# A convolution norm with its low parts on VectorE, its gates' sigmoids in one piece and the Silu table loaded ahead; a last norm whose gain is multiplied in half by half

## The chip, the cores and the metric

The kernel runs on one core of a Trainium2 chip. A core has TensorE (PE, with its weight loads shown apart as PEld), VectorE (DVE), ScalarE (ACT), GpSimd (POOL), SyncE (SP, which issues the transfers here) and 16 DMA engines. The metric is the device time of one execution in microseconds. The kernel before took 1084.35 us in the median of three runs (1084.35, 1085.1 and 1082.03). A fourth execution was profiled.

## The reference, cut to what matters

A sequence of 256 tokens of width 1024 in float32 passes one hybrid block (attention, a matrix LSTM and an MLP) and then two layers of a second block. The change touches the second block and the norm behind it:

```python
for l in range(2):
    h = rms_norm_2(x, norm1_g[l]) * (1.0 + scale1) + shift1
    z = h @ w_in[l]
    ...
    y_attn = o.reshape(b, s, ATTN_W) @ w_attn_o[l]
    ga, gb = jnp.split(z[..., C_OFF:G_OFF], 2, axis=-1)
    u = ga * jax.nn.sigmoid(gb)
    u = causal_depthwise_conv(u, dw_conv_w[l], dw_conv_b[l])       # 31 taps, 512 channels
    u = jax.nn.silu(layer_norm(u, conv_ln_g[l], conv_ln_b[l]))
    y_conv = u @ w_conv_o[l]
    g_attn, g_conv = jnp.split(jax.nn.sigmoid(z[..., G_OFF:]), 2, axis=-1)
    mixed = (g_attn * y_attn + g_conv * y_conv) @ w_out[l]
    x = x + (1.0 + gate1) * mixed
    h2 = rms_norm_2(x, norm2_g[l]) * (1.0 + scale2) + shift2
    f_gate, f_up = jnp.split(h2 @ w_ffn_in[l], 2, axis=-1)
    x = x + (1.0 + gate2) * ((jax.nn.silu(f_gate) * f_up) @ w_ffn_out[l])
return rms_norm_2(x, final_g)
```

`rms_norm_2` multiplies by the reciprocal root of the mean of the squares and by a gain; `layer_norm` does so after taking off the mean, and adds a bias.

## The kernel before, in words

Every large product runs as three TensorE passes over float32 parts. A weight piece of 128x1024 is loaded as `raw`; ScalarE copies it to a rounded high part `whi` (L202), and the low part `wlo` = raw minus high part is made by GpSimd (L206) or VectorE (L208). Which of the two is settled when the program is written out, by a running sum in `split`: each piece adds `rot["pool"]` to `rot["n"]`; when the sum reaches 1, the piece goes to GpSimd and 1 is taken off, else to VectorE. With `rot["pool"]` at 0.75 every fourth piece goes to VectorE, with 1.0 none. Activations are split in the same way, high part on ScalarE (L589), low part on VectorE (L590).

Order. Each engine runs its own instructions in the order in which the Python program writes them; semaphores join the engines. The program writes TensorE's blocks, and after each block `tick()` gives a turn to queues of generators: `fills`, `bg`, and `pump()`, which splits the next weight pieces while fewer than 9 (`HB`) are ahead of their use. A `yield` in a generator means: the rest is written after a later block.

The second block, per layer: q, k, v and the gates' products; the attention in `attention2()` beside them; the depthwise convolution `conv()` as a `bg` generator, 31 taps on VectorE (L1251); then the four blocks "ao" (w_attn_o), the four blocks "co" (w_conv_o), then w_out, a norm, and the FFN.

The gates. The products leave the gates' input in the tile `gt` (called T in the trace), copied there at L1387. `sig(j)` (L1391) is one ScalarE sigmoid over a quarter of it, 128x1024. Two of them stand ahead of the ao blocks, the third ahead of ao block 1, the fourth ahead of ao block 2 (`SIG = (1, 2)`). After each ao block VectorE multiplies the gate into the result (L1398).

The convolution's norm, at the end of `conv()`, is written in turns between the ao blocks: mean by TensorE with a matrix of ones, mean taken off on VectorE (L1262), squares on ScalarE (L1266), their sum by TensorE (L1272), plus eps on VectorE (L1275), power -0.5 on GpSimd (L1276: "the root"), two diagonal matrices from it on ScalarE (L1279), a product with ones on TensorE that spreads the root over the partitions (L1285), four products on VectorE (L1287), and Silu on ScalarE (L1293). L589 and L590 then split the result into `uT` (called AB in the trace), which the co blocks read (TensorE L288 to L290). Between sigmoid and Silu ScalarE loads another table, an instruction of its own (ACT_TABLE_LOAD) that stands ahead of the first function that needs it. When the taps are done, `conv()` sets `rot["pool"]` from 1.0 to `LN_POOL`, 0.75.

The end. `end_all()` runs for each of two tiles of 128 tokens after the last product: per half of 512 columns gate product (L565), residual sum (L566), squares with their sum (L506); then on GpSimd eps and root (L498, L499), on VectorE x times root times `final_g` for both halves (L1468), each followed by its transfer out (L1469).

Of the kernel before, what the change touches and what calls it, by code (L numbers as in the profile page):

```python
# [43 lines left out]
TAPS_AT = 2  # L44
LOADS = 3
LN = (1, 2, 2)
SIG = (1, 2)
FDEL, ZDEL = 2, 3
RED, ROWD = 5, 8
ATT = (0, 1, 2, 4, 5, 6, 7)  # L50
# [7 lines left out]
def tile_hybrid_then_diff(ctx: ExitStack, tc: tile.TileContext, I, out: bass.AP):  # L58
# [17 lines left out]
    def st_tile():  # L76
        return sb.tile([128, 8], FT, name="st", bufs=12)

    def xn_tile(shape=(128, 1024)):
        return sb.tile(list(shape), FT, name="xn", bufs=2)  # L80
# [421 lines left out]
    def halves_of(v):  # L502
        return [v[:, n * 512:(n + 1) * 512] for n in range(2)]
# [58 lines left out]
    def post_gate(t, acc, grow, xn, sx):  # L562
        xs, g = halves_of(x[t]), halves_of(grow)
        for n in range(2):
            V.tensor_mul(acc[n], acc[n], g[n])  # L565
            V.tensor_add(xs[n], xs[n], acc[n])  # L566
            square(t, n, xn(), sx)
            if n == 0:
                yield
# [651 lines left out]
    for l in range(NL):  # L1221
        cu = sb.tile([128, 4, 286], FT, name="cu")
        G.memset(cu[:, :, 0:30], 0.0)
        attended = []
        uT = []

        def evac(t, acc):
# [14 lines left out]
        def conv():  # L1242
# [9 lines left out]
                                           cw[:, l * 4 + j, k:k + 1], sums[j], op0=OP.mult, op1=OP.add)  # L1252
                    yield
            rate["bg"] = 1
            rot["pool"] = LN_POOL
            s3 = xn_tile((128, 4, 256))
            for _ in range(LN[0]):
                yield
# [18 lines left out]
            dg = s3[:, 3, :]  # L1277
            for t in range(2):
                A.activation(dg[:, t * 128:(t + 1) * 128], ident, AF.Copy, scale=st[:, 2 + t:3 + t])  # L1279
            for _ in range(LN[2]):  # L1280
                yield
            while not attended:
# [106 lines left out]

        def sig(j):  # L1390
            A.activation(gt[:, 4 * j:4 * j + 4, :], gt[:, 4 * j:4 * j + 4, :], AF.Sigmoid)  # L1391

        sig(0)
        sig(1)
        for j in range(4):
            if j in SIG:
                sig(2 + SIG.index(j))
            b4_half("ao", oT, lambda ps, j=j: V.tensor_mul(gt[:, 2 * j:2 * j + 2, :], gt[:, 2 * j:2 * j + 2, :], ps))  # L1398
        drain_q(bg)
        rot["pool"] = POOL  # L1400
# [59 lines left out]
            yield from fin(post_gate, t, acc, g2[0], gc, bc)  # L1460

        def end_all(t, acc):
            st = st_tile()
            o = xn_tile()
            yield from post_gate(t, acc, g2[0], lambda: o, st)
            rstd2(st[:, 2:3], st, 1e-6)
            for n, (v, u, g) in enumerate(zip(halves_of(x[t]), halves_of(o), halves_of(gfin))):
                V.scalar_tensor_tensor(u, v, st[:, 2:3], g, op0=OP.mult, op1=OP.mult)  # L1468
                nc.sync.dma_start(out[0, t * 128:(t + 1) * 128, n * 512:(n + 1) * 512], u)  # L1469
            yield  # L1470

        ffn(FF2 // 256, PRE2, prefix2, up2, "fo", end_all if l == NL - 1 else to_layer(l + 1, end_layer),
# [28 lines left out]
```

## Time and profile before

| | |
|---|---|
| runs | 1084.35, 1085.1, 1082.03 us |
| profiled execution, time | 1083.16 us |
| its span in the trace | 1081.4 us |
| instructions | 17255 |
| DMA | 231.84 MB, mean 214 GB/s |

The profile covers one execution, from its first to its last instruction; 1.8 us of the execution's own time lie outside the span. In rows of the timeline the columns are: start and duration in us, engine, line, operation, output<-input by the program's names, shape; a count x2 after several equal instructions in a row, whose duration is then that of all; in brackets the idle time of the engine ahead of it and what ended that. Busy shares of engines that others don't wait for say nothing of the end. [...]

### The profile page before, as it was taken

What the parts mean: (1) busy time and instruction counts of PE and PEld (TensorE: products, weight loads), DVE (VectorE), ACT (ScalarE), POOL (GpSimd) and SP (SyncE); (2) the same over time, 40 slices, a digit from 0 to 9 for tenths busy, and PEclk for the clock granted to TensorE, in tenths of its full rate; (3) what the DMA queues carried; (4) which work ended last, traced back from release to release, by engine and by line L of the source; (5) the groups of instructions that cost most, each with busy time, mean ns of one, the idle gap of its engine ahead of it and who ended that gap; (6) DMA issues with size and microseconds to landing.
All of it is one profiled execution on the core that took longest, in us unless ns stands there. A gap on an engine that the chain in (4) does not pass through costs nothing.

```text
span 1081.4 us, 17255 instructions
## 1 busy us (share of the span) xinstructions
PE 1036.0 (96%) x6459; PEld 917.6 (85%) x6459; DVE 647.9 (60%) x1161; ACT 558.8 (52%) x933; POOL 691.5 (64%) x424
## 2 busy tenths in 40 slices
PE   8879989999998999989999999999999899999997
PEld 6667769899886789988798998888899778999995
DVE  4536556887854497834679797547873554441224
ACT  5745746444455556665643434475676545443441
POOL 2474648566575797846656665859967458566661
PEclk9989999999999999999999999999999999999999
DMA  8554545999974565546499999837635456765631
GB/s 259 169 176 130 192 146 189 345 356 362 329 268 136 167 185 165 187 156 175 132 353 318 332 343 358 299 104 214 186 127 175 137 175 224 258 224 180 198 108 39
DMA packets 169424, 231.84 MB, mean 214 GB/s; under 512 B 10215, under 2 KB 109757, under 8 KB 169339
## 3 DMA queue, kind: packets, MB, share of 16 engines
q1 hardware_dynamic: 169211, 230.71, 65.0%
q8 instruction: 51, 0.84, 0.3%
q14 instruction: 34, 0.28, 0.1%
q0 software_dynamic: 128, 0.02, 0.0%
HBM read 229.64 MB, written 1.06 MB: 213 GB/s over the span
## 4 chain that ended last, share of the span: by engine, by line
PE 75%; POOL 8%; DVE 6%; ACT 6%; issue 3%; DMA 2%; POOLq 0%; SPq 0%; DVEq 0%; ACTq 0%
PE bank L288 17%; PE bank L289 17%; PE bank L290 17%; PE bank L300 12%; POOL wlo L206 6%; PE bank L302 6%; ACT whi L202 2%; DVE bank L762 2%; DVE wlo L208 2%; DMA raw<-in_ada_w_dram 2%; PE bank L840 1%; ACT xn L506 1%; PE bank L860 1%; PE bank L531 1%; PE bank L832 0%
## 5 line engine op out<-in xcount | busy, mean ns | idle before, releaser
L206 POOL TENSOR_TENSOR wlo<-raw,whi 128x1024 fp32r<-128x1024 f32 x255 | 631.5, 2498 | 259.1 <-ACT whi L202 228.4
L202 ACT ACTIVATE whi<-raw 128x1024 fp32r<-128x1024 f32 x332 | 337.4, 1054 | 78.3 <-DMA raw<-in_w_down_dram 30.6
L288 PE MATMUL bank<-T,whi 128*128 128x256 f32 x1072 | 307.7, 287 | 2.3 <-DVE sc L773 2.3
L290 PE MATMUL bank<-T,wlo 128*128 128x256 f32 x1072 | 303.4, 283 | 0.0
L289 PE MATMUL bank<-T,whi 128*128 128x256 f32 x1072 | 303.3, 283 | 0.0
L288 PEld LDWEIGHTS bank<-T,whi 128*128 128x128 f32 x1072 | 205.1, 191 | 6.8 <-issue 3.7
L289 PEld LDWEIGHTS bank<-T,whi 128*128 128x128 f32 x1072 | 205.2, 191 | 1.1
L290 PEld LDWEIGHTS bank<-T,wlo 128*128 128x128 f32 x1072 | 205.1, 191 | 0.0
L300 PE MATMUL bank<-whi,T 128*128 128x512 f32 (+1 forms) x672 | 185.0, 398 | 7.3 <-ACT T L589 4.7
L208 DVE TENSOR_TENSOR wlo<-raw,whi 128x1024 fp32r<-128x1024 f32 x77 | 125.5, 1630 | 100.6 <-ACT whi L202 100.1
L300 PEld LDWEIGHTS bank<-whi,T 128*128 128x128 f32 x672 | 123.9, 192 | 36.6 <-ACT T L589 6.1
L762 DVE SCALAR_TENSOR_TENSOR bank<-raw,cact,bank 128x512 f32<-128x512 f32 x168 | 126.9, 755 | 7.5 <-DMA raw<-in_ada_w_dram 2.1
L288 PE MATMUL bank<-whi,AB 128*128 128x512 f32 x304 | 120.7, 397 | 0.0
L290 PE MATMUL bank<-whi,AB 128*128 128x512 f32 x304 | 120.1, 395 | 0.0
L289 PE MATMUL bank<-wlo,AB 128*128 128x512 f32 x304 | 120.0, 395 | 0.0
L302 PE MATMUL bank<-wlo,T 128*128 128x512 f32 (+1 forms) x336 | 103.8, 393 | 4.0 <-POOL wlo L206 3.0
L1251 DVE SCALAR_TENSOR_TENSOR bank<-cu,cw,bank 128x256 f32<-128x256 f32 x232 | 104.4, 486 | 4.2
L302 PEld LDWEIGHTS bank<-wlo,T 128*128 128x128 f32 x336 | 62.4, 190 | 19.9 <-POOL wlo L206 4.3
L589 ACT ACTIVATE AB<-bank 128x512 fp32r<-128x512 f32 (+1 forms) x49 | 26.0, 537 | 91.3 <-DVE bank L1449 66.2
L290 PEld LDWEIGHTS bank<-whi,AB 128*128 128x128 f32 x304 | 57.3, 188 | 13.4
L288 PEld LDWEIGHTS bank<-whi,AB 128*128 128x128 f32 x304 | 57.4, 189 | 12.0
L289 PEld LDWEIGHTS bank<-wlo,AB 128*128 128x128 f32 x304 | 57.3, 189 | 12.0
(283 smaller groups left out, 1160.5 us busy)
## 6 DMA issues: line engine op xcount, KB each, us to landing
raw<-in_w_in_dram SPq DMA_DIRECT2D x96, 512.0 KB
raw<-in_ada_w_dram SPq DMA_DIRECT2D x96, 512.0 KB
raw<-in_w_ffn_in_dram SPq DMA_DIRECT2D x88, 512.0 KB
raw<-in_w_ffn_out_dram SPq DMA_DIRECT2D x44, 512.0 KB
raw<-in_w_up_dram SPq DMA_DIRECT2D x32, 512.0 KB
raw<-in_w_down_dram SPq DMA_DIRECT2D x32, 512.0 KB
raw<-in_w_out_dram SPq DMA_DIRECT2D x24, 512.0 KB
raw<-in_w_attn_o_dram SPq DMA_DIRECT2D x8, 512.0 KB
```

What stands on the lines that cost most here:

```text
L202: A.activation(hi, r, AF.Copy)
L206: G.tensor_sub(lo, r, hi.bitcast(FT))
L208: V.tensor_sub(lo, r, hi.bitcast(FT))
L288: T.matmul(o, lh, rh, start=start, stop=False)
L289: T.matmul(o, lh, rl, start=False, stop=False)
L290: T.matmul(o, ll, rh, start=False, stop=stop)
L300: T.matmul(o, xT[:, a, k0 + kk, ts], w[0][:, kk, cs], start=start and kk == a == 0, stop=False)
L302: T.matmul(o, xT[:, 0, k0 + kk, ts], w[1][:, kk, cs], start=False, stop=stop and kk == kn - 1)
L506: A.activation(halves_of(xn)[n], halves_of(x[t])[n], AF.Square, scale=1.0 / 32, accum_out=st[:, n:n + 1])
L589: A.activation(dst_hi, full, AF.Copy)
L762: V.scalar_tensor_tensor(ada["sum"], r[:, kk, :], cact[:, k:k + 1], ada["sum"], op0=OP.mult, op1=OP.add)
L1251: V.scalar_tensor_tensor(ca[:, j, :] if k == 30 else sums[j], cu[:, j, k:k + 256], cw[:, l * 4 + j, k:k + 1], sums[j], op0=OP.mult, op1=OP ...
```

## The change

Four edits.

1. `SIG` is gone. The four sigmoids stand one behind the other ahead of the first ao block; each notes itself in a list `gated`.
2. After the taps `rot["pool"]` is 0.0 instead of 0.75, so that each low part is VectorE's (and the running sum `rot["n"]` stands still), until the diagonal matrices are written; from there on 0.75.
3. Behind the diagonal matrices `conv()` waits (in the order of writing) until four sigmoids are in `gated`, and then writes a Silu of one column of ones into an unused column of `st`. It brings the Silu table's load to this place.
4. `end_all()` is written anew: `final_g` is multiplied into half 0 as soon as that half of x is there; eps is added to half 0's sum of squares; with half 1's sum there is one addition and the root. ScalarE scales half 0 by the root, VectorE half 1 by root and gain, and both transfers are issued after these.

```diff
-SIG = (1, 2)
...
         attended = []
+        gated = []
         uT = []
...
             rate["bg"] = 1
-            rot["pool"] = LN_POOL
+            rot["pool"] = 0.0
             s3 = xn_tile((128, 4, 256))
...
             for t in range(2):
                 A.activation(dg[:, t * 128:(t + 1) * 128], ident, AF.Copy, scale=st[:, 2 + t:3 + t])
+            rot["pool"] = LN_POOL
+            while len(gated) < 4:
+                yield
+            A.activation(st[:, 4:5], ones[:, 0:1], AF.Silu)
             for _ in range(LN[2]):
                 yield
...
         def sig(j):
             A.activation(gt[:, 4 * j:4 * j + 4, :], gt[:, 4 * j:4 * j + 4, :], AF.Sigmoid)
-
-        sig(0)
-        sig(1)
+            gated.append(j)
+
         for j in range(4):
-            if j in SIG:
-                sig(2 + SIG.index(j))
+            sig(j)
+        for j in range(4):
             b4_half("ao", oT, lambda ps, j=j: V.tensor_mul(gt[:, 2 * j:2 * j + 2, :], gt[:, 2 * j:2 * j + 2, :], ps))
...
         def end_all(t, acc):
-            st = st_tile()
-            o = xn_tile()
-            yield from post_gate(t, acc, g2[0], lambda: o, st)
-            rstd2(st[:, 2:3], st, 1e-6)
-            for n, (v, u, g) in enumerate(zip(halves_of(x[t]), halves_of(o), halves_of(gfin))):
-                V.scalar_tensor_tensor(u, v, st[:, 2:3], g, op0=OP.mult, op1=OP.mult)
-                nc.sync.dma_start(out[0, t * 128:(t + 1) * 128, n * 512:(n + 1) * 512], u)
+            st, o, junk = st_tile(), xn_tile(), sc_tile()
+            xs, os, gs, fs = (halves_of(v) for v in (x[t], o, g2[0], gfin))
+            for n in range(2):
+                V.tensor_mul(acc[n], acc[n], gs[n])
+                V.tensor_add(xs[n], xs[n], acc[n])
+                A.activation(junk, xs[n], AF.Square, scale=1.0 / 32, accum_out=st[:, n:n + 1])
+                if n == 0:
+                    V.tensor_mul(os[0], xs[0], fs[0])
+                    G.tensor_scalar(st[:, 3:4], st[:, 0:1], 1e-6, None, op0=OP.add)
+                    yield
+            G.tensor_add(st[:, 4:5], st[:, 3:4], st[:, 1:2])
+            G.tensor_tensor(st[:, 5:6], st[:, 4:5], nhalf[:, 0:1], op=OP.pow)
+            A.activation(os[0], os[0], AF.Copy, scale=st[:, 5:6])
+            V.scalar_tensor_tensor(os[1], xs[1], st[:, 5:6], fs[1], op0=OP.mult, op1=OP.mult)
+            for n in range(2):
+                nc.sync.dma_start(out[0, t * 128:(t + 1) * 128, n * 512:(n + 1) * 512], os[n])
             yield
```

What this does to the order of the instructions is shown at three places. In the changed file lines up to the gates have numbers one lower (L201, L205 and L207 for the high part and for the low part on GpSimd and on VectorE), the sigmoids are L1395, the early Silu is L1283, the products by the root L1291, the gate products L1401 and the Silu itself L1297. Numbers after an underscore tell buffers apart; the piece from raw_4568 is the same in both.

ScalarE in layer 0, from the last copy of the gates' input to the first Silu, before and changed:

```order
L1391 ACT_TABLE_LOAD
L1391 ACTIVATE T16_4062<-T16_4062 128x1024 x2
L202 ACTIVATE whi_4844<-raw_4562 128x1024
L1279 ACTIVATE xn_4776<-ident_113,st_4859 128x128 x2
L1391 ACTIVATE T16_4062<-T16_4062 128x1024
L202 ACTIVATE whi_4891<-raw_4568 128x1024
L1391 ACTIVATE T16_4062<-T16_4062 128x1024
L202 ACTIVATE whi_4924<-raw_4654 128x1024
L202 ACTIVATE whi_4962<-raw_4660 128x1024
L1293 ACT_TABLE_LOAD
L1293 ACTIVATE bank_4970<-xn_3765,col_157 128x256 x2
```

```order
L1395 ACT_TABLE_LOAD
L1395 ACTIVATE T16_4062<-T16_4062 128x1024 x4
L201 ACTIVATE whi_4846<-raw_4562 128x1024
L1279 ACTIVATE xn_4776<-ident_113,st_4861 128x128 x2
L1283 ACT_TABLE_LOAD
L1283 ACTIVATE st_4861<-ones_101 128x1
L201 ACTIVATE whi_4893<-raw_4568 128x1024
L201 ACTIVATE whi_4925<-raw_4654 128x1024
L201 ACTIVATE whi_4963<-raw_4660 128x1024
L1297 ACTIVATE bank_4971<-xn_3765,col_157 128x256 x2
```

Two sigmoids went from behind the diagonal matrices to ahead of the second weight piece. The table's load went from just ahead of Silu to behind the matrices, with three weight pieces between it and Silu. Layer 1 has the same order.

VectorE in layer 0, from the mean's subtraction on, before and changed:

```order
L1262 SCALAR_TENSOR_TENSOR xn_3765<-bank_4777,xn_3765 128x1024
L1398 TENSOR_TENSOR T16_4062<-T16_4062,bank_4818 128x512
L1275 TENSOR_SCALAR st_4859<-bank_4850 128x2
L1398 TENSOR_TENSOR T16_4062<-T16_4062,bank_4865 128x512
L208 TENSOR_TENSOR wlo_4892<-raw_4568,whi_4891 128x1024
L1398 TENSOR_TENSOR T16_4062<-T16_4062,bank_4898 128x512
L1287 TENSOR_TENSOR xn_3765<-xn_3765,bank_4930 128x256 x4
```

```order
L1262 SCALAR_TENSOR_TENSOR xn_3765<-bank_4777,xn_3765 128x1024
L207 TENSOR_TENSOR wlo_4811<-raw_4468,whi_4810 128x1024
L1401 TENSOR_TENSOR T16_4062<-T16_4062,bank_4820 128x512
L207 TENSOR_TENSOR wlo_4847<-raw_4562,whi_4846 128x1024
L1275 TENSOR_SCALAR st_4861<-bank_4852 128x2
L1401 TENSOR_TENSOR T16_4062<-T16_4062,bank_4867 128x512
L1401 TENSOR_TENSOR T16_4062<-T16_4062,bank_4899 128x512
L1291 TENSOR_TENSOR xn_3765<-xn_3765,bank_4931 128x256 x4
```

Two low parts have come ahead of the addition of eps (L1275), the second of them from the weight piece that ScalarE splits after its four sigmoids. The one ahead of the products by the root is gone; in layer 0 the next low part on VectorE stands behind those products.

The same stretch of VectorE in layer 1, before and changed:

```order
L1398 TENSOR_TENSOR T16_7944<-T16_7944,bank_8768 128x512
L208 TENSOR_TENSOR wlo_8795<-raw_8524,whi_8794 128x1024
L1287 TENSOR_TENSOR xn_7647<-xn_7647,bank_8800 128x256 x4
L1398 TENSOR_TENSOR T16_7944<-T16_7944,bank_8806 128x512
L590 TENSOR_TENSOR AB_8839<-bank_8840,AB_8838 128x512
```

```order
L207 TENSOR_TENSOR wlo_8718<-raw_8433,whi_8717 128x1024
L1275 TENSOR_SCALAR st_8732<-bank_8723 128x2
L1401 TENSOR_TENSOR T16_7945<-T16_7945,bank_8738 128x512
L1401 TENSOR_TENSOR T16_7945<-T16_7945,bank_8770 128x512
L207 TENSOR_TENSOR wlo_8797<-raw_8525,whi_8796 128x1024
L1291 TENSOR_TENSOR xn_7648<-xn_7648,bank_8802 128x256 x4
L1401 TENSOR_TENSOR T16_7945<-T16_7945,bank_8808 128x512
L589 TENSOR_TENSOR AB_8841<-bank_8842,AB_8840 128x512
```

In layer 1 a low part stays ahead of the products by the root. It belongs to the second of the three weight pieces that ScalarE now splits behind the table's load; the first and the third of them are GpSimd's.

The orders of TensorE and SP are the same in both files but for names.

## Rows read from the trace of the kernel before

**Rows 1.** The page's first part: busy time, share of the span and instructions of each engine.

```profile
PE 1036.0 (96%) x6459; PEld 917.6 (85%) x6459; DVE 647.9 (60%) x1161; ACT 558.8 (52%) x933; POOL 691.5 (64%) x424
```

**Rows 2.** The waits of TensorE by what ended them, the first of them: total us, times, the longest.

```profile
PE bank L288 <- ACT AB L589: 7.8, 2, 3.9
```

**Rows 3.** Timeline of ScalarE in layer 0, from the sigmoids' table to the first two Silus.

```profile
462.50 1.28 ACT L1391 ACT_TABLE_LOAD   x1
463.79 2.01 ACT L1391 ACTIVATE T<-T 128x1024 f32<-128x1024 f32 x2
465.70 1.04 ACT L202 ACTIVATE whi<-raw 128x1024 fp32r<-128x1024 f32 x1
469.90 0.70 ACT L1279 ACTIVATE xn<-ident,st 128x128 f32<-128x128 f32 x2 [3.15 <-POOL st L1276]
470.50 1.04 ACT L1391 ACTIVATE T<-T 128x1024 f32<-128x1024 f32 x1
471.45 1.04 ACT L202 ACTIVATE whi<-raw 128x1024 fp32r<-128x1024 f32 x1
...
473.35 1.98 ACT L202 ACTIVATE whi<-raw 128x1024 fp32r<-128x1024 f32 x2
475.35 1.28 ACT L1293 ACT_TABLE_LOAD   x1
476.64 1.17 ACT L1293 ACTIVATE bank<-xn,col 128x256 f32<-128x256 f32 x2
```

**Rows 4.** Timeline of VectorE in layer 0: the addition of eps, the low part, the products by the root, the low part of the activations.

```profile
465.49 0.15 DVE L1275 TENSOR_SCALAR st<-bank 128x2 f32<-128x2 f32 x1
...
472.58 1.23 DVE L208 TENSOR_TENSOR wlo<-raw,whi 128x1024 fp32r<-128x1024 f32 x1 [3.42 <-ACT whi L202]
...
474.32 1.41 DVE L1287 TENSOR_TENSOR xn<-xn,bank 128x256 f32<-128x256 f32 x4
```

**Rows 5.** Timeline of GpSimd in layer 0, around the root.

```profile
466.82 2.40 POOL L206 TENSOR_TENSOR wlo<-raw,whi 128x1024 fp32r<-128x1024 f32 x1 [1.90 <-ACT whi L202]
469.17 0.69 POOL L1276 TENSOR_TENSOR st<-st,nhalf 128x2 f32<-128x2 f32 x1
```

**Rows 6.** Timeline of ScalarE in layer 1, from the diagonal matrices to the first two Silus.

```profile
835.31 0.69 ACT L1279 ACTIVATE xn<-ident,st 128x128 f32<-128x128 f32 x2 [3.15 <-POOL st L1276]
...
840.76 1.28 ACT L1293 ACT_TABLE_LOAD   x1
842.06 1.17 ACT L1293 ACTIVATE bank<-xn,col 128x256 f32<-128x256 f32 x2
```

**Rows 7.** Timelines of VectorE and of GpSimd in layer 1, the low parts ahead of the products by the root.

```profile
839.89 1.58 DVE L208 TENSOR_TENSOR wlo<-raw,whi 128x1024 fp32r<-128x1024 f32 x1 [2.38 <-ACT whi L202]
841.39 1.40 DVE L1287 TENSOR_TENSOR xn<-xn,bank 128x256 f32<-128x256 f32 x4
```

```profile
837.98 2.41 POOL L206 TENSOR_TENSOR wlo<-raw,whi 128x1024 fp32r<-128x1024 f32 x1 [2.70 <-ACT whi L202]
```

**Rows 8.** Timelines of VectorE and of GpSimd late in the last FFN, where a low part on each runs at the same time.

```profile
1054.64 2.59 DVE L208 TENSOR_TENSOR wlo<-raw,whi 128x1024 fp32r<-128x1024 f32 x1 [1.20 <-ACT whi L202]
```

```profile
1053.74 2.40 POOL L206 TENSOR_TENSOR wlo<-raw,whi 128x1024 fp32r<-128x1024 f32 x1 [1.78 <-ACT whi L202]
```

**Rows 9.** Busy time (and instructions) of each engine in stretches of the span, with the granted clock (PEclk), the DMA share and GB/s: the stall ahead of the co blocks and the stretch behind it, in layer 0 and in layer 1, and the stretches behind two shorter stalls.

```profile
474.60:478.40 3.80, 0.00 (x0) 0.00 (x0) 1.72 (x5) 3.70 (x6) 3.80 (x2) 1.00 0.53 159
478.40:482.90 4.50, 3.92 (x16) 3.43 (x17) 1.38 (x2) 1.67 (x4) 0.72 (x1) 0.62 0.86 304
843.90:848.20 4.30, 3.91 (x16) 3.42 (x17) 1.37 (x2) 1.58 (x3) 0.00 (x0) 0.60 0.84 292
151.40:155.20 3.80, 3.80 (x9) 2.85 (x10) 3.22 (x8) 2.60 (x9) 0.39 (x2) 0.55 0.60 209
883.10:887.10 4.00, 4.00 (x16) 3.10 (x17) 3.48 (x9) 1.62 (x5) 0.00 (x0) 1.00 0.79 300
```

**Rows 10.** Timeline of TensorE: the first instructions behind those two shorter stalls.

```profile
151.38 2.10 PE L300 MATMUL bank<-whi,T 128*128 128x512 f32 x4 [1.97 <-ACT T L589]
```

```profile
883.09 1.20 PE L300 MATMUL bank<-whi,T 128*128 128x512 f32 x3 [2.03 <-ACT T L589]
```

**Rows 11.** Timeline of the end of the span, all engines.

```profile
1073.62 0.70 DVE L565 TENSOR_TENSOR bank<-bank,row 128x512 f32<-128x512 f32 x1 [2.35 <-PE bank L290]
...
1075.61 0.19 ACT L506 ACTIVATION_READ_ACCUMULATOR xn<-x 128x1 f32 x1
1075.89 0.30 POOL L498 TENSOR_SCALAR st<-st 128x1 f32<-128x1 f32 x1 [7.41 <-ACT xn L506]
1076.28 0.56 POOL L499 TENSOR_TENSOR st<-st,nhalf 128x1 f32<-128x1 f32 x1
1076.87 1.42 DVE L1468 SCALAR_TENSOR_TENSOR xn<-x,st,vt 128x512 f32<-128x512 f32 x2 [1.83 <-POOL st L499]
1077.65 0.99 SPq L1469 DMA_DIRECT2D out_dram<-xn  x2
```

**Rows 12.** One line's instructions over the span, minimum, median and maximum in ns: ScalarE's scaling of a half by a column.

```profile
L512 ACT ACTIVATE xn<-x,st x10: 722/724/732, 145.0 to 890.3; 128x512 f32<-128x512 f32 x10
```

**Rows 13.** The FFN of layer 0: VectorE's low parts from 540 to 690 us (count, busy us, mean ns, idle before), and busy times of all engines in one stretch of it.

```profile
L208 DVE TENSOR_TENSOR wlo<-raw,whi 128x1024 fp32r<-128x1024 f32 x13 | 19.3, 1487 | 4.9 <-ACT whi L202 4.9
```

```profile
620.00:640.00 20.00, 20.00 (x136) 18.41 (x134) 18.77 (x25) 9.20 (x10) 12.87 (x6) 1.00 0.99 354
```

## The prediction

> **What bounds the kernel now.** I read the page first: TensorE is busy for 1036.0 of 1081.4 us [rows 1], so an edit on the other engines can only touch the 45 us in which it waits, or stretches in which it runs at its lower clock. The view of TensorE's waits comes next: its largest entry belongs to this change, two waits of 3.9 us for the high part of the convolution's result, 7.8 us together [rows 2]. One lies ahead of the co blocks in each layer; there TensorE does nothing from 474.6 to 478.4 [rows 9]. Then I read backwards in the timelines what ends those waits. In layer 0 Silu starts at 476.64, right behind its table's load (475.35 and 1.28), and that right behind two weight pieces; from the diagonal matrices at 469.90 on ScalarE has no gap, so its own queue sets the end: matrices to Silu take 6.74 us [rows 3]. The matrices wait for the root, which GpSimd starts at 469.17, as a low part begun at 466.82 ends [rows 5]. The sum behind the root was ready far sooner, since eps was added at 465.49 [rows 4]. Layer 1 has the same rows 365.4 us later. The third place is the end: root, two products on VectorE, two transfers [rows 11].
>
> The trace's own execution took 1083.16 us, 1.8 more than its span. The runs' median is 1084.35, and the mean of all four executions shown is 1083.66. A measurement of this kernel tells a change from none from about 0.3%, 3.25 us, on.
>
> **Layer 0, the root.** The change takes the low part away from ahead of the root on GpSimd, but puts two on VectorE ahead of the addition of eps. The second of them needs the high part that ScalarE now makes behind four sigmoids. Sigmoids start at 463.79 and pass at 0.955 each (2.01 for two, the next instruction at 465.70), so four end at 467.61 and the weight piece (1.04) at 468.65 [rows 3]. VectorE starts a low part 0.09 behind its high part (471.45 + 1.04 against 472.58) and takes 1.23 where GpSimd is still [rows 3, 4], as it is here, its queue holding nothing else ahead of the root: 469.97. Eps (0.15) starts in its last 0.09 as other rows do and ends at 470.03; the root starts at 470.10, against 469.17, 0.93 later. So the root is not made earlier: what it waited for on GpSimd has been exchanged for a wait on VectorE behind ScalarE. Queued behind eps on VectorE are gate products and the products by the root, and TensorE waits for neither before the co blocks.
>
> **Layer 0, root to Silu.** Matrices at 469.90 + 0.93 = 470.83. Then ScalarE has: matrices 0.60, the table 1.29, the early Silu of one column, three weight pieces. No row shows a Silu of one column; its bounds are nothing and 0.5 us (half a Silu of 256 columns, 1.17 for two), and I take 0.19, the shortest of ScalarE's rows at hand [rows 11]. Pieces pass at 1.00 (two from 473.35 to 475.35). Sum 0.60 + 1.29 + 0.19 + 3.00 = 5.08, so Silu at 475.91 instead of 476.64: a gain of 0.73 [rows 3]. This is the two sigmoids (1.9) less the later root and the early Silu. The table's load is not hidden by being early: ScalarE waits for nothing between matrices and Silu, before or after, so that its place among them is worth nothing. VectorE's four products take 1.41 [rows 4] behind the spread root (some 472.1), end at 473.6, and don't hold Silu. The next low part of VectorE stands behind them.
>
> **Layer 1.** The same shift sets the matrices at 835.31 + 0.93 = 836.24, the table's end at 838.13, the weight pieces at 838.32, 839.30 and 840.28, so ScalarE alone would be ready at 841.3. But the second piece's low part is VectorE's, and the products by the root are queued behind it. Its high part is there at 840.34. GpSimd begins the first piece's low part at 839.44 (838.32 + 1.04 + 0.08) and takes 2.41 [rows 7], to 841.85. What a low part on VectorE does at such a time stands in the trace: one that was begun at 1054.64, 0.90 after GpSimd's, took 2.59 instead of 1.23 and ended 1.09 after GpSimd's end [rows 8]; that in layer 1 before was held too, 1.58 [rows 7]. So I put its end at 841.85 + 1.09 = 842.94, the first product by the root at 842.85 (it takes 0.35, a quarter of 1.40) and Silu at 843.3 instead of 842.06 [rows 6]: a loss of 1.25. Bounds: not held, ScalarE decides, a gain of 0.73; held, and each of the four products held as well behind GpSimd's third piece (2.4 more), a loss of 3.6. I stay at 1.25, the row nearest in kind.
>
> [...]
>
> **The end.** The extra product of half 0 lies in VectorE's idle time of 2.35 ahead of the last half [rows 11]. Addition and root on GpSimd are two small instructions as before, so the root ends at 1076.84 again. Before, two products took 1.42 one after the other, and the second transfer was issued some 0.67 behind the first. Now both halves are scaled side by side, ScalarE in 0.72 [rows 12], VectorE in 0.71, both done at about 1077.6, and SP's issues of about 0.34 each (0.99 for two with a gap) follow one another: the second 0.43 earlier than before. It stays between nothing (the second transfer waits behind the first) and 0.67 (both go at once). I take 0.43.
>
> **Elsewhere.** Two pieces fewer raise the running sum in each layer, so that in the FFN of layer 0 VectorE's low parts move by two pieces; one in four stays its share. There VectorE is busy for 18.77 of 20 us [rows 13], yet no more work comes to it. I cost it at nothing, since TensorE has up to nine pieces ahead; without that cover each held low part costs up to 1.36 (2.59 less 1.23).
>
> **Sum.** -0.73 + 1.25 - 0.43 = +0.1 us, on 1083.16, or on the four executions' mean 1083.7. The clock stands apart from it. Behind both stalls TensorE runs at a granted 0.62 over 4.5 us and 0.60 over 4.3 us [rows 9], which is 1.7 us lost each time (4.5 x 0.38; 4.3 x 0.40). The stall in layer 0 falls by 0.73, and by 0.4 more as TensorE itself waits for the later spread of the root, from 3.92 to about 2.8. Of shorter stalls, one of 2.03 was followed by 1.00 and one of 1.97 by 0.55 [rows 9, 10], so length alone doesn't tell, and I leave both losses in.
>
> **The rivals.**
> 1. *The clock holds in layer 0.* For it: 2.03 without a fall. Against it: 1.97 with one. It would give back 1.7: 1082.0.
> 2. *VectorE's low part in layer 1 isn't held*, because its high part comes before GpSimd starts, or GpSimd is late. Then layer 1 gains 0.73 too: -0.73 - 0.73 - 0.43 = -1.9, time 1081.8; with the clock kept in both layers 3.4 less, 1078.4. For it: a margin of only 0.9 between the two starts. Against it: rows 7 and 8, and GpSimd's piece is the first of the three.
> 3. *Slower: low parts in the FFN of layer 0 meet GpSimd's.* VectorE has 13 of them there, and their mean of 1487 ns shows that some are held already [rows 13]. If the shift by two pieces puts more of them behind GpSimd's, each costs 1.36 in a stage where VectorE has 1.2 us of 20 free. The first is absorbed by that, and it decides from the fourth on (three more on the path are 4.1): with five in all 5.4 us, 1089.1. Against it: weight pieces ahead.
> 4. *The change doesn't do what it says about the root:* it does come early, because the sigmoids or the second piece wait for less than I think. Root back at 469.17: each layer gains 0.93 more on ScalarE, layer 1 still waits for VectorE, and its low part, held all the same, ends 0.93 earlier: 1083.7 - 1.9 = 1081.8.
>
> **How the numbers follow.** Forecast 0.58, rival 1 0.18, rival 2 0.12, rival 3 0.06, rival 4 0.06. All but rival 3 and the clock's part of rival 2 lie within 3.25 us of the median. Faster by over 0.3%: half of rival 2, and 0.07 for gains of the others that add up: 0.13. Slower: rival 3 and 0.01 for the upper bound in layer 1: 0.07. Within: 0.80. The likeliest time is the sum on the four executions' mean, 1083.7. The range goes from 1081.0 (rivals 1, 2 and 4, less the 0.8 by which runs stray) to 1086.2 (the upper bound in layer 1, 2.4 above the forecast).
>
> **What would show it.** In the profile after: the root's start at about 470.1 instead of 469.2; Silu at about 475.9 in layer 0 and 843.3 in layer 1 (less what layer 0 gives); VectorE's low part in layer 1 at 2.4 to 2.6 us; TensorE's waits ahead of the co blocks of about 2.8 and 4.8 us instead of 3.9 twice; the granted clock behind them at about 0.6; the last transfer's issue 0.4 earlier behind the last matmul. A low part of 1.2 us in layer 1, or a clock of 1.00 behind either stall, would show the forecast wrong on the fast side; new waits of TensorE for low parts between 540 and 690 us on the slow side.

## The result, and the profile after

The changed kernel takes 1094.12 us in the median of five runs (1090.26 to 1095.61), beside 1084.87 of the kernel before: a ratio of 1.0085 (95% interval 1.0068 to 1.0102). It is slower by some 9 us, and the time lies outside the range of the prediction. The profiled execution is the longest of the five: 1095.61, with a span of 1093.9. One execution of all that follow, of the second of the two other sets below, ran slow at 2029.86 us, and its ratio is taken without it.

TensorE has 6459 matmul records in both traces, in the same order, so that each can be set beside its partner. The lag below is the start after less the start before; the two gaps are TensorE's idle time just ahead of that matmul, before and after.

```
start before   lag   gap before / after   what ended the wait after
   440.01    -0.35      -
   478.49    -1.23     3.92 / 2.46        ScalarE, high part of the convolution's result (layer 0)
   516.07    -1.26      -
   526.68    -2.37     0.93 / 0.00        (a wait for a low part that is gone)
   527.71    -1.69      -
   588.24    +0.40     1.50 / 3.32        VectorE, transposition L772
   589.65    +1.50      -
   663.93    +3.94     0.79 / 2.98        VectorE, transposition L772
   667.22    +6.50      -
   710.45    +7.22     0.00 / 0.55        ScalarE, high part L588
   719.57    +9.49     0.00 / 1.25        GpSimd, low part L205
   762.45   +10.28     0.00 / 0.62        GpSimd L825
   843.91   +11.55     3.92 / 4.61        ScalarE, high part of the convolution's result (layer 1)
   848.99   +12.25      -
   894.49   +12.65     0.87 / 0.00
```

Between 516 and 762 the lag grows from -1.26 to +10.28: 11.5 of the 12.5 us lie in the FFN of layer 0 and the norm behind it, where the change writes no edit. Layer 0's norm gains, layer 1's loses some 2 us. The waits of TensorE after (total, times, longest) have a new large entry beside the one of [rows 2]: VectorE's transposition, 6.3 us in two waits. The same wait was 2.3 us before (first fence: a row of before that the prediction didn't show; second: after).

```profile
PE bank L288 <- DVE sc L773: 2.3, 2, 1.5
```

```profile
PE bank L287 <- ACT AB L588: 7.1, 2, 4.6
PE bank L287 <- DVE sc L772: 6.3, 2, 3.3
...
PE bank L301 <- POOL wlo L205: 2.5, 2, 1.3
```

The stretches of the span behind these waits (busy time and instructions of each engine, granted clock, DMA share, GB/s), which answer to [rows 9], show what a wait costs besides. The granted clock is a share of TensorE's full clock; between 440 and 930 us of both profiles it is 1.00 but for stretches of 3.41 or 6.83 us at 0.50 (before from 479.43 and 844.66; after from 479.07, 588.30, 666.80, 854.54 and 895.50), and 3.41 us at 0.50 are 1.7 us lost. Behind 588 and 667, where the profile before has 1.00 throughout (580 to 600 and 660 to 680 us), TensorE is granted 0.54 and 0.57. Behind layer 1's stall it is 0.51 over 6.1 us, which is 3.0 us lost, where it was 0.60 over 4.3 us, 1.7 lost. That last difference is not one of the kernel alone: a second profile of the changed kernel, whose stall there is again 4.61, has 0.64 over 6.1 us (second fence), 2.2 lost.

```profile
477.30:482.40 5.10, 4.43 (x19) 3.74 (x20) 1.33 (x2) 1.54 (x3) 2.09 (x1) 0.67 0.66 204
588.60:592.00 3.40, 3.36 (x16) 3.36 (x17) 3.27 (x5) 0.66 (x1) 3.40 (x2) 0.54 0.93 304
667.90:674.50 6.60, 6.60 (x34) 6.60 (x35) 4.44 (x9) 1.06 (x1) 5.32 (x3) 0.57 1.11 352
...
855.40:861.50 6.10, 5.86 (x24) 5.27 (x25) 1.38 (x2) 1.63 (x4) 0.05 (x1) 0.51 0.70 243
```

```profile
856.90:863.00 6.10, 5.84 (x30) 5.25 (x31) 1.85 (x3) 1.64 (x4) 0.07 (x1) 0.64 0.74 252
```

Layer 0's norm, timelines of VectorE, GpSimd and ScalarE after, beside [rows 3 to 5]. The second low part ends at 469.60, eps and root follow, and the matrices stand at 470.48.

```profile
468.38 1.22 DVE L207 TENSOR_TENSOR wlo<-raw,whi 128x1024 fp32r<-128x1024 f32 x1 [3.16 <-ACT whi L201]
469.52 0.15 DVE L1275 TENSOR_SCALAR st<-bank 128x2 f32<-128x2 f32 x1
```

```profile
469.75 0.69 POOL L1276 TENSOR_TENSOR st<-st,nhalf 128x2 f32<-128x2 f32 x1 [9.23 <-DVE st L1275]
```

```profile
470.48 0.69 ACT L1279 ACTIVATE xn<-ident,st 128x128 f32<-128x128 f32 x2 [2.19 <-POOL st L1276]
471.19 1.28 ACT L1283 ACT_TABLE_LOAD   x1
472.48 0.20 ACT L1283 ACTIVATE st<-ones 128x1 f32<-128x1 f32 x1
472.59 2.94 ACT L201 ACTIVATE whi<-raw 128x1024 fp32r<-128x1024 f32 x3
475.43 1.15 ACT L1297 ACTIVATE bank<-xn,col 128x256 f32<-128x256 f32 x2
```

The same in layer 1, VectorE and then ScalarE, beside [rows 6, 7]: the low part is held to 2.49, the products by the root come behind it, and Silu waits 2.00 for them.

```profile
850.75 2.49 DVE L207 TENSOR_TENSOR wlo<-raw,whi 128x1024 fp32r<-128x1024 f32 x1 [3.00 <-ACT whi L201]
853.16 1.40 DVE L1291 TENSOR_TENSOR xn<-xn,bank 128x256 f32<-128x256 f32 x4
```

```profile
853.60 1.17 ACT L1297 ACTIVATE bank<-xn,col 128x256 f32<-128x256 f32 x2 [2.00 <-DVE xn L1291]
```

The end, beside [rows 11]: both halves are scaled side by side from 1089.43, and both transfers go from 1090.17.

```profile
1089.43 0.72 ACT L1478 ACTIVATE xn<-xn,st 128x512 f32<-128x512 f32 x1 [1.02 <-POOL st L1477]
1089.43 0.75 DVE L1479 SCALAR_TENSOR_TENSOR xn<-x,st,vt 128x512 f32<-128x512 f32 x1 [1.84 <-POOL st L1477]
1090.17 0.81 SPq L1481 DMA_DIRECT2D out_dram<-xn  x2
```

And VectorE's low parts in the FFN of layer 0 after, beside the first of [rows 13]: the same count of 13, but 21.8 us instead of 19.3, and 8.1 us of waiting for high parts instead of 4.9. Those of 13 that take over 1.4 us are five before (1.47 to 2.58) and four after (1.86 to 3.22).

```profile
L207 DVE TENSOR_TENSOR wlo<-raw,whi 128x1024 fp32r<-128x1024 f32 x13 | 21.8, 1674 | 8.1 <-ACT whi L201 8.1
```

What stands around 667 us? Beside the FFN VectorE multiplies ada_w, the weights from which scales, shifts and gates come, and adds the products up in a bank, one of the buffers that TensorE writes its own sums to. A transposition on VectorE (L773 before, L772 after) reads the finished sum and sets the bank free, and TensorE waits for that. Timeline of VectorE before, and after:

```profile
659.91 3.13 DVE L762 SCALAR_TENSOR_TENSOR bank<-raw,cact,bank 128x512 f32<-128x512 f32 x4 [0.53 <-DMA raw<-in_ada_w_dram]
663.07 0.72 DVE L773 STREAM_TRANSPOSE sc<-bank 128x512 f32<-128x512 f32 x1
```

```profile
661.64 3.13 DVE L761 SCALAR_TENSOR_TENSOR bank<-raw,cact,bank 128x512 f32<-128x512 f32 x4 [1.24 <-DMA raw<-in_ada_w_dram]
665.88 1.23 DVE L207 TENSOR_TENSOR wlo<-raw,whi 128x1024 fp32r<-128x1024 f32 x1 [1.11 <-ACT whi L201]
667.02 0.71 DVE L772 STREAM_TRANSPOSE sc<-bank 128x512 f32<-128x512 f32 x1
```

Before, the transposition follows the last sum at once. After, a low part stands between, waits 1.11 for its high part and takes 1.23. Some 17 us ahead of the wait at 588 there is another (VectorE, then GpSimd, after): a low part held to 3.05 by GpSimd's, which began 0.42 sooner, ahead of four sums.

```profile
571.11 3.05 DVE L207 TENSOR_TENSOR wlo<-raw,whi 128x1024 fp32r<-128x1024 f32 x1
```

```profile
570.69 2.38 POOL L205 TENSOR_TENSOR wlo<-raw,whi 128x1024 fp32r<-128x1024 f32 x1 [1.54 <-ACT whi L201]
```

### The profile page after: what moved, and what is told of

Same layout as the page of the kernel before. It is cut to its first block, busy times and chain, and to the rows that moved or that the text cites. A ratio compares the mean times of both kernels' runs of the same rounds, so it can differ in the third digit from the quotient of the medians.

```text
span 1093.9 us, 17258 instructions
## 1 busy us (share of the span) xinstructions
PE 1043.3 (95%) x6459; PEld 923.2 (84%) x6459; DVE 653.7 (60%) x1164; ACT 560.1 (51%) x937; POOL 684.7 (63%) x423
## 4 chain that ended last, share of the span: by engine, by line
PE 67%; POOL 10%; DVE 7%; ACT 6%; issue 6%; DMA 3%; POOLq 0%; SPq 0%; ACTq 0%; DVEq 0%
PE bank L287 17%; PE bank L288 17%; PE bank L289 17%; PE bank L299 8%; POOL wlo L205 7%; PE bank L301 4%; ACT whi L201 2%; DVE wlo L207 2%; DMA raw<-in_w_ffn_in_dram 2%; DVE bank L761 1%; PE bank L839 1%; ACT xn L505 1%; DMA raw<-in_w_in_dram 1%; DMA raw<-in_w_ffn_out_dram 1%; DVE bank L536 1%
## 5 line engine op out<-in xcount | busy, mean ns | idle before, releaser
L205 POOL TENSOR_TENSOR wlo<-raw,whi 128x1024 fp32r<-128x1024 f32 x252 | 624.2, 2500 | 254.9 <-ACT whi L201 225.6
L201 ACT ACTIVATE whi<-raw 128x1024 fp32r<-128x1024 f32 x332 | 336.8, 1054 | 86.9 <-DMA raw<-in_w_ffn_in_dram 34.8
L207 DVE TENSOR_TENSOR wlo<-raw,whi 128x1024 fp32r<-128x1024 f32 x80 | 134.5, 1682 | 116.4 <-ACT whi L201 115.1
```

The lines of the kernel that those rows point to most:

```text
L201: A.activation(hi, r, AF.Copy)
L205: G.tensor_sub(lo, r, hi.bitcast(FT))
L207: V.tensor_sub(lo, r, hi.bitcast(FT))
```

## The experiments

Each ratio is to runs of the kernel before on the same chip. Theory A: the loss comes from which low parts are VectorE's in the FFN of layer 0 and the norm behind it. Theory B: it comes from TensorE arriving there early, at work that is no earlier.

**The old set put back.** The changed kernel with

```diff
             rot["pool"] = LN_POOL
+            rot["n"] = rot["n"] + 0.5 if l == 0 else 0.25
             while len(gated) < 4:
```

> The changed kernel, but behind the diagonal matrices of layer 0 half a unit is added to the running sum, so that from the co blocks of layer 0 to the norm of layer 1 each weight piece's low part goes to the engine that had it before; in layer 1's norm and from there on all is as in the changed kernel. Theory A (the loss comes from which low parts are VectorE's in the FFN of layer 0 and in the norm behind it): the lag of TensorE behind the kernel before no longer grows between 540 and 830 us, where it grew by some 11.4 us; time about 1086.3 (1084.9, less 0.9 in layer 0's norm, plus 2.0 in layer 1's and 0.3 behind it). Theory B (the loss comes from TensorE being early there, so that it meets transfers and VectorE's sums that are no earlier): the waits at 588 and 667 us stay, time about 1094.

1084.91, ratio 1.0018 (1.0007 to 1.003). Nothing is left of the growing lag between 516 and 762 us, and no wait at 588 or 667 is longer than before (1.51 and 0.29). That is what theory A foretold. It does not refute B, since TensorE is not early here (its lag is +0.17 at 527); the next kernel does.

**The new set alone.** The kernel before with

```diff
             rot["pool"] = LN_POOL
+            if l == 1:
+                rot["n"] = 0.75
...
         drain_q(bg)
         rot["pool"] = POOL
+        if l == 0:
+            rot["n"] += 0.5
```

> The kernel before, but with half a unit added to the running sum behind the ao blocks of layer 0 and the old value set again in layer 1's convolution, so that in the FFN of layer 0 and in the norm behind it VectorE has the low parts that it has in the changed kernel; nothing else differs. Theory A: the two waits of TensorE for VectorE's transposition at 588 and 667 us and the waits at 718 to 730 us appear here too, time about 1096 (1084.9 + 11.2). Theory B: about 1085.

1095.37, ratio 1.0119 (1.0099 to 1.0138): the whole loss, without any of the four edits as such. TensorE waits 3.32 at 591 and 3.24 at 671 us, for the same transposition (from its list of waits, beside 2.3 in the kernel before). It is not early here (its lag is +0.6 at 527), so that theory B falls.

```profile
PE bank L288 <- DVE sc L773: 6.6, 2, 3.3
```

**The held low part of layer 1.** As the first, with `rot["n"] += 0.5` in both layers.

> As the first of these kernels, but with half a unit added in layer 1 too: there the one low part that stood ahead of the products by the root on VectorE (2.49 us, held by GpSimd) becomes GpSimd's, and no other piece changes. Theory A with the held low part as the cause of layer 1's loss: Silu waits only for ScalarE's queue, 2.0 us earlier, and the stall ahead of the co blocks falls from 4.6 to about 2.6; 1084.2, and 1.7 less where the clock behind the stall then stays low for one window less: about 1082.5. If instead the table's load or the later root cost the time in layer 1: the same as the first kernel.

1082.49, ratio 0.9997 (0.9985 to 1.0008). It differs from the first in one piece, and both stalls ahead of the co blocks are now 2.51 (the first had 4.61 in layer 1): the held low part, not the table's load or the root, was layer 1's loss (TensorE's list of waits, the first kernel and this one).

```profile
PE bank L287 <- ACT AB L588: 7.1, 2, 4.6
```

```profile
PE bank L287 <- ACT AB L588: 5.0, 2, 2.5
```

Behind that stall TensorE is granted 0.69 over 5.55 us, against 0.50 over 5.4 in the first kernel: 1.7 us lost instead of 2.7. That part can't be put down to the piece, for in layer 0, where the two kernels are alike, it is 1.7 lost against 3.4 behind stalls of 2.51 and 2.47. Against the kernel before, the norm's edits and the end together are worth nothing that can be measured, though both stalls are 1.4 shorter. By the trace TensorE waits 0.28 for the matrices ahead of each stall, leaves the stall only 0.9 earlier than before, and has lost 0.5 to 0.6 of that again by 516 and 849 us.

**The new end alone**, on the kernel before.

> The kernel before with the new end alone (final_g on half the result early, both halves scaled side by side). My prediction: 0.43 us less. By the trace of the changed kernel, whose second transfer is issued 4.81 us behind the last matmul instead of 5.02: 0.05 to 0.2 less. In either case the time is the same within the measurement, about 1084.7.

1083.68, ratio 1.0005 (0.9991 to 1.0018): no gain to be seen.

**Single pieces.** The changed kernel, with the engine of single pieces set apart from the running sum:

```diff
-        if rot["n"] >= 1.0:
+        pool = rot["n"] >= 1.0
+        if pool:
             rot["n"] -= 1.0
+        rot["made"] = rot.get("made", -1) + 1
+        if FORCE.get(rot["made"], pool):
             G.tensor_sub(lo, r, hi.bitcast(FT))
```

with FORCE = {202: True}, then {218: True, 220: False}, then {170: True}.

> The changed kernel with one weight piece of the FFN of layer 0 given to the other engine: the low part that VectorE makes at 665.9 us, between its last sum and the transposition that frees the bank for which TensorE waits at 667.9, is GpSimd's; the running sum goes on as if nothing had changed. Theory A1 (a low part ahead of a transposition holds it): the transposition follows the last sum at once, 2.25 us earlier (1.11 of waiting and 1.2 of work), TensorE's wait falls from 2.98 to about 0.7, and the low clock behind it (666.8 to 673.6, 2.6 us lost) goes or halves: time 1089.2 to 1091.9. Rival A2 (the transfers of ada_w set it): the wait stays, time about 1094.

1091.48, ratio 1.0076 (1.0059 to 1.0093). In the timeline of VectorE the transposition follows the sum at once:

```profile
661.56 3.13 DVE L765 SCALAR_TENSOR_TENSOR bank<-raw,cact,bank 128x512 f32<-128x512 f32 x4 [1.60 <-DMA raw<-in_ada_w_dram]
664.72 0.72 DVE L776 STREAM_TRANSPOSE sc<-bank 128x512 f32<-128x512 f32 x1
```

TensorE's lag to the changed kernel, -0.84 just ahead of the wait, is -2.29 at its end and -4.85 at 674 us, since the clock is 1.00 over the next 6.4 us. The wait is 1.53, more than the 0.7 expected: VectorE's last sums waited 1.60 for the transfer of ada_w (first row), so that rival A2 holds for this rest.

> The changed kernel with two pieces exchanged in the norm behind the FFN of layer 0: the low part that VectorE makes at 713.8 us, held to 2.59 by GpSimd, goes to GpSimd, and the one of 726.6, which GpSimd makes there ahead of a second, goes to VectorE, as in the kernel before. Theory A1: the three waits of TensorE at 717 to 729 us (0.55, 0.21, 1.25) and the small one at 772 go, and the lag grows by some 3 us less there: about 1091. Rival: the waits move to other pieces, about 1094.

1091.64, ratio 1.0069 (1.0054 to 1.0084). The three waits of TensorE at 717 to 729 are gone, and the lag to the changed kernel goes from -0.11 at 674 us to -3.10 at 729. The small wait at 772, expected to go as well, stays (0.67).

> The changed kernel with the low part that VectorE makes at 571.1 us, held to 3.05 by GpSimd, given to GpSimd. Theory A1: VectorE's sums, and with them the transposition at 587.9 for which TensorE waits 3.32, come up to 3 us earlier, the wait falls to between 0.3 and 1.5 and the low clock behind it (588.3 to 591.7, 1.4 us lost) goes: 1090.9 to 1092.3. Rival: VectorE has the time back before 588 because it waits for ada_w there: about 1094.

1090.1, ratio 1.0054 (1.0039 to 1.0069). The wait at 588 falls from 3.32 to 0.70, and the clock behind it is 1.00 over 4.0 us. The transposition stands at 585.73 instead of 587.87 (VectorE, the changed kernel and this one):

```profile
587.87 0.72 DVE L772 STREAM_TRANSPOSE sc<-bank 128x512 f32<-128x512 f32 x1
```

```profile
585.73 0.72 DVE L776 STREAM_TRANSPOSE sc<-bank 128x512 f32<-128x512 f32 x1
```

By the whole time the first two can't be told from the changed kernel, whose interval theirs overlap, and the third hardly; what shows their part is the place in the trace. So the three were put together, beside the changed kernel once more:

> The changed kernel with the three exchanges of single pieces together (the low parts of 571.1 and 665.9 us given to GpSimd, the two of the norm behind the FFN of layer 0 exchanged); twenty other pieces of that stretch stay where the changed kernel has them, other than in the kernel before. If the three places account for the loss: no wait of TensorE above 1.5 us between 540 and 770 us, and the time of the kernel with the whole set put back, a ratio of 1.002 to kernel before. If the set as a whole costs: half of the loss or more stays, a ratio of 1.005 or above.

> The changed kernel once more, beside the one above on the same chip: the ratio of 1.0085 (1.0068 to 1.0102) again; the kernel before with only its low parts moved came to 1.0119 (1.0099 to 1.0138), so that something up to 1.011 would not surprise.

The changed kernel came to 1095.74, ratio 1.0106 (1.0089 to 1.0124), and with the three exchanges to 1082.87, ratio 0.9987 (0.9975 to 0.9999). The wait for the transposition is down to 1.8 us in two places (TensorE's list of waits), and TensorE comes through 588 with 1.2 us in hand, which speaks against theory B once more.

```profile
PE bank L291 <- DVE sc L776: 1.8, 2, 1.1
```

The engines of four pieces are the loss, as far as the time can tell; of the rest of the set the trace still shows the wait at 762 us (0.66). This kernel is even 2 us below the first, where the old set was put back whole, 1082.87 beside 1084.91. Between 516 and 762 us their profiles differ by only 0.35 us, so that the difference lies elsewhere; its cause was not looked for.

**The early root.** The third kernel, with the sum of squares, eps and root one block sooner:

```diff
-LN = (1, 2, 2)
+LN = (1, 1, 2)
...
             G.tensor_tensor(st[:, 2:4], st[:, 0:2], nhalf[:, 0:2], op=OP.pow)
+            yield
             dg = s3[:, 3, :]
```

> The changed kernel with half a unit added in both layers (as in the earlier kernel that came to 1082.5) and with the sum of squares, eps and the root written one block earlier, ahead of the second low part on VectorE, the diagonal matrices where they were. If the root is late because eps is queued behind a low part that waits for ScalarE's four sigmoids: ScalarE's idle time of 2.2 us ahead of the matrices goes, Silu comes 2.2 earlier and the stall ahead of the co blocks falls from 2.5 to about 0.5 in each layer: 1082.5 - 4.0 = 1078.5, and with the full clock behind both stalls 3.4 less, 1075. If ScalarE's work itself is the end: 1082.5.

1075.01, ratio 0.9918 (0.9903 to 0.9933). That it is the number expected to the microsecond is partly luck: the stalls fell by 1.7 each, not by 2.0. GpSimd makes the root at 462.50, and ScalarE (second fence, timeline of layer 0) reaches the matrices with no idle time:

```profile
462.50 0.69 POOL L1276 TENSOR_TENSOR st<-st,nhalf 128x2 f32<-128x2 f32 x1 [3.07 <-DVE st L1275]
```

```profile
466.16 1.04 ACT L201 ACTIVATE whi<-raw 128x1024 fp32r<-128x1024 f32 x1
467.11 0.68 ACT L1280 ACTIVATE xn<-ident,st 128x128 f32<-128x128 f32 x2
467.80 1.28 ACT L1285 ACT_TABLE_LOAD   x1
...
472.05 1.15 ACT L1299 ACTIVATE bank<-xn,col 128x256 f32<-128x256 f32 x2
```

Both stalls ahead of the co blocks are 0.81, and behind both the clock stays at 1.00 (stretches of the span as above):

```profile
473.90:478.00 4.10, 3.30 (x21) 2.70 (x22) 1.35 (x2) 1.55 (x3) 3.48 (x2) 1.00 0.85 240
...
835.20:839.30 4.10, 3.30 (x21) 2.70 (x22) 1.36 (x2) 1.57 (x3) 3.48 (x2) 1.00 0.78 239
```

**The table late.** That kernel without the early Silu (`-A.activation(st[:, 4:5], ones[:, 0:1], AF.Silu)`).

> The kernel with the early root (1075.0) without the early Silu of one column, so that the Silu table is loaded right ahead of Silu again. My prediction's step (ScalarE has no gap between matrices and Silu, so the place of the load among its instructions is worth nothing): Silu 0.1 to 0.2 earlier, by the early Silu's own time; time 1074.5 to 1075.2. If loading ahead hides the table: up to 1.3 later in each layer, about 1077.6 and more with the low clock.

1074.68, ratio 0.9907 (0.9886 to 0.9928): the same time. Where the load stands is worth nothing here, where ScalarE has no gap between matrices and Silu; that was the prediction's step.

**The two other sets.** The early root with another quarter of the running sum (`rot["n"] += 0.25 if l == 0 else 0.75`; then 0.75 in layer 0 and `rot["n"] = 1.25` in layer 1).

> The kernel with the early root, with 0.25 added to the running sum in layer 0 instead of 0.5, and 0.75 in layer 1 so that behind that all is alike: in the FFN of layer 0 and the norm behind it VectorE's low parts are those one weight piece beside. Theory A1 (what counts is whether a low part lies ahead of a sum or a transposition whose bank TensorE waits for, not how many there are): another time than 1075.0, since other pieces are VectorE's, between 1075 and 1086 (the loss of 11 of the changed kernel's set); where it is within 1 us, neither of the two sets holds a transposition.

> As the one before, with 0.75 added in layer 0 and layer 1's sum set so that all is alike behind it: the fourth of the possible sets in the FFN of layer 0. Theory A1: between 1075 and 1086 by the same argument. If every set but that of the kernel before costs about 11, it would be a matter of the whole stage, and not of single pieces.

1083.03, ratio 0.9986 (0.9974 to 0.9999), and 1088.55, ratio 1.0043 (1.0028 to 1.0059), against 0.9918 with the old set. They lose 8 and 13 us, and the second is beyond the 11 that I set as its end. Both have a wait of TensorE of over 4 us for the transposition between 585 and 590 us, where the old set has 1.51, one of 2.59 and 1.79 at 665 and 669 us, put down to ScalarE, where it has 0.84, and one of 1.1 to 1.25 for a low part in the norm behind the FFN. In which piece each loss lies was not tried.

**The early root alone**, on the kernel before (the diff of the kernel of that name above, and nothing else).

> The kernel before with the one edit of the early root: the sum of squares, eps and the root written one block earlier, the matrices where they were. None of the four edits of the change is in it. If what holds Silu is ScalarE's idle time of 3.15 us ahead of the matrices, all of it goes: the two stalls fall from 3.9 to about 0.8, 1083.7 - 6.3 = 1077.4, and 3.4 less with the full clock behind them, 1074. Then the change's own edits in the norm aren't needed for the gain of the kernel with the early root. If they are: about 1080 or more, with layer 1's held low part (1.58 us) as what is late next.

1074.48, ratio 0.9909 (0.9892 to 0.9925). Timeline of ScalarE in layer 0, where [rows 3] had 3.15 of idle time:

```profile
465.34 1.04 ACT L202 ACTIVATE whi<-raw 128x1024 fp32r<-128x1024 f32 x1
466.29 0.68 ACT L1280 ACTIVATE xn<-ident,st 128x128 f32<-128x128 f32 x2
...
471.74 1.28 ACT L1294 ACT_TABLE_LOAD   x1
473.03 1.17 ACT L1294 ACTIVATE bank<-xn,col 128x256 f32<-128x256 f32 x2
```

The stalls are 0.74 and 0.87, two of the 53 of the last section behind which no low clock came. Two lines on the kernel before are as fast as all the edits with them; no kernel here is faster beyond the noise than this one, some 10 us under the kernel before, and it has none of the change's edits.

## Why the prediction was wrong

The step that failed is the part "Elsewhere": "I cost it at nothing, since TensorE has up to nine pieces ahead". Pieces ahead do cover late low parts in the FFN: from 530 to 695 us TensorE waits for no low part in the profile after. But what TensorE waits for there are banks that VectorE's transpositions set free, and a low part is queued ahead of these on VectorE, so nothing that TensorE has ahead covers it. The profile before showed it: the wait for L773 stood in the list of waits, 2.3 us in two places, and I read of that list only its first entry. So the set of pieces was worth 11.5 us by the lag, and I gave it 0.

Rival 3 had the right place and the right sign at a chance of 0.06. Its price of 5.4 (1089.1) was too low and its mechanism only half of it. By this profile the loss has four parts: low parts held by GpSimd (3.05 at 571; 2.59 in the norm), a low part that waits for its high part ahead of a transposition (2.25 at 667), two low parts of the norm one after the other on GpSimd instead of one on each engine (a wait of 1.25), and the low clock behind the two new waits (1.6 us at 0.54 over 3.4, 2.8 us at 0.57 over 6.6). I named the first alone. Its count was wrong too: I asked whether more low parts would be held, and of the 13 those of over 1.4 us went from five to four; what counted was what stood behind them.

Right, point by point:

- The root in layer 0. Predicted for 470.10; it starts at 469.75 in an execution that runs 0.35 ahead there. It is not made earlier than before, as the prediction said, and for the reason given. Rival 4 is refuted by this row.
- Silu in layer 0 at 475.91; measured 475.43, with the 0.35 added 475.78. The early Silu takes 0.20 (0.19 taken).
- Silu in layer 1 at 843.3; measured 853.60, less the lag of 10.31 there 843.29. The low part takes 2.49 (2.4 to 2.6 foreseen). Rival 2 is refuted here, and the third kernel shows that this low part is the cause.
- The products by the root aren't held for themselves: they take 1.40 in layer 1 while GpSimd works on two low parts (first row below, timeline of GpSimd after), and 1.42 in layer 0 (start 471.96) with GpSimd idle, so that the loss stayed at 1.25 and the bound of 3.6 was none. In the profile before it was so as well: 1.41 in layer 0 [rows 4] beside a low part that GpSimd begins at 474.46 (second row, timeline of GpSimd before).

```profile
849.79 5.67 POOL L205 TENSOR_TENSOR wlo<-raw,whi 128x1024 fp32r<-128x1024 f32 x2 [3.27 <-ACT whi L201]
```

```profile
474.46 4.66 POOL L206 TENSOR_TENSOR wlo<-raw,whi 128x1024 fp32r<-128x1024 f32 x2 [4.60 <-ACT whi L202]
```

- The waits ahead of the co blocks: 2.46 and 4.61, foreseen as 2.8 and 4.8.
- The clock fell behind the stall in layer 0 although it was shorter, against rival 1. In layer 1 I left the loss as it was; in this profile the longer stall was followed by 0.51 over 6.1 us, which costs 3.0 instead of 1.7. I had no term for that, but none goes by the stall's length: behind the same stall of 4.61 seven profiles lost between 1.7 and 3.2.
- The place of the table's load is worth nothing, shown by the early root without the early Silu.

The end was mis-sized: 0.43 foreseen, but the second issue ends 4.81 us behind the start of the last half on VectorE instead of 5.02, and the span from there to its end is 7.73 instead of 7.75. The first transfer gains nothing, since it waits for root and one scaling as before; alone the new end can't be told from the old.

Without the shift of the set, and so without the missed term, the time would have lain in the range: the first kernel came to 1084.91. That is still 1.5 over the kernel before beside it (1083.42), where I had +0.1; in its profile the clock behind the two stalls lost 3.4 and 2.8 us, where I had 1.7 each.

## What to carry to other kernels

Where a running sum deals work out between engines, an edit that skips two steps of it moves every later piece; compare the order of the engines far behind the edit, and hold the sum as it was when the edit is to be judged. A low part that is cheap by its own time is priced by what is queued behind it on its engine: look in the list of waits for the engines that release TensorE's banks, however small the entry, before calling a stage covered. And before trading work among engines for a late value, look whether the value can simply be written earlier: here its inputs were there a block before, and two lines gave what four edits did not.

## What was not expected of the hardware

The cost of a wait went on behind it. In the sixteen profiles TensorE has 35 stalls of 2.46 to 4.61 us between 440 and 930 us, and each came with a stretch at the low clock, 1.4 to 3.4 us lost; 17 of 2.03 to 2.06 did so six times, and 53 of 0.70 to 1.79 never. In the kernel before these are two of 3.92 (1.7 lost behind each) and one of 2.03 (1.00 over 4.0 us, [rows 9]); in the changed one 2.46, 3.32, 2.98 and 4.61 (1.7, 1.6, 2.8 and 3.0 lost) and one of 2.03, behind which it is 0.57 over 4.0 us. Among the 35 the loss did not go by the length: stalls of 2.46 to 2.51 lost 1.7 to 3.4, those of 4.61 1.7 to 3.2. Two cuts of 1.7 us each, of stalls that were 2.5 and came down to 0.81, so brought 7.5 us (1082.49 to 1075.01).

How long a low part on VectorE was held went by when it began. In the kernel before, 32 begin while GpSimd makes one; 29 of them end 1.08 to 1.09 us after GpSimd's does, so that one begun 0.33 behind takes 3.15 us and one begun 2.02 behind 1.47, instead of 1.23; the other three begin 2.35 behind or later and aren't held (1.21 to 1.23). GpSimd's took up to 3.47 (at 695.43) instead of 2.4 where it began behind VectorE's.
